# S5 matrices of a diffusion-transformer step: powers and B spread over partitions by DMA instead of transposes on TensorE

## Chip, cores and metric

One core of a Trainium2 chip runs the whole kernel in one launch. The metric is the time of one execution in device microseconds (us). A core has five engines that run side by side, each in the fixed order of its own instruction list: TensorE (PE, with PEld for its weight loads), VectorE (DVE), ScalarE (ACT), GpSimd (POOL) and SyncE (SP), which here issues nearly all DMAs.

## What is computed

The reference is one step of a four-layer backbone for 128 context and 512 latent tokens of width 1024. Layers 0 and 3 mix tokens by windowed attention, layer 2 by full attention, layer 1 by a bidirectional S5 layer; after each mixer stands a gated convolutional feed-forward network (FFN, width 2816). Each sub-layer is scaled, shifted and gated by a linear map of the conditioning ("modulation"). Of the S5 layer, cut to what matters here:

```
dt = exp(log_dt); mag = exp(lam_re*dt)
a  = mag * (cos(lam_im*dt) + i sin(lam_im*dt))      # per direction, 64 groups x 64 states
f  = (a - 1) / lam
bb = f * B                                          # 64 states x 16 channels, complex
h_t = a * h_(t-1) + bb @ u_t                        # scan forward, and a second one backward
y  = u*d_skip + sum over directions of Re(C h)
```

The kernel doesn't scan token by token. It works in chunks of eight tokens, and for this needs, per direction d and block of four group pairs (blk), matrices made of the powers a^0 to a^8 times bb or times C: an input matrix W (`d_w1`: from the 8 x 16 inputs of a chunk to the 64 complex states), an output matrix (`d_w3`, from P = C times powers) and a Toeplitz part inside the chunk (`d_kx`, from P times bb).

## The kernel before

Activations X lie in SBUF with channels on partitions. Every dense product is done in three f32 passes (`mm3`, L297 to L299): weights and inputs are split into a high and a low part, and hi*hi, hi*lo and lo*hi are added up. Weights come from DRAM through a pool of three raw tiles (`raw`, 1 MB each); ACT writes the high part `wh` (L302), DVE the low part `wl` (L306). PSUM tiles come from two pools, `psa` (two tiles) and `psb` (four banks). The build's scheduler fixes the order of each engine once; at run time each engine and each DMA queue goes through its list in that order and waits on semaphores. SP's list holds the weight loads, the loads and writes of the S5 work, and everything between.

The matrices of layer 1 don't depend on activations, and are made ahead, as side work between the matmuls of layer 0:

- `s5_param_steps` (a generator, three steps per chunk of w_o) runs in `project_out` of layer 0, about 306 to 365 us in the trace. It makes a and f for 64 (direction, pair) rows x 128 columns (`four`), transposes them on PE to 128 partitions, builds the powers `pw` (a^0 to a^8) by complex products (`cmul`, L1107 to L1113) on DVE, computes `bb` on DVE, and gathers powers, transposed C and bb in the tile `par`, one 392-wide row per step, written to DRAM as `d_par` (L1241). The last step loads the S5 start state and transposes it on PE (L1245, L1247).
- `s5_matrices` runs in `ffn` of layer 0, about 365 to 850 us, mixed three stages to one with the modulation products of the next layer. A step is one (blk, d), sixteen in all, each of four stages. Stage one loads `s5par` (L1265), makes P on DVE (real part) and POOL (imaginary part), three operations each (L1278 to L1280), writes it to `d_w3` (L1283) and builds the block-diagonal `bz` on ACT (L1292). Stage two multiplies P and bz on PE (L1299, eight products). Stage three copies the result to `kx`, and makes Q = bb times powers, three operations each on DVE and POOL (L1320 to L1322); Q lies state by input, and stands in the buffers that P had. Stage four transposes Q on PE (L1328, eight transposes of 128x128), and ACT evicts the four groups into W (L1331, with the sign of the imaginary part), which one DMA writes to `d_w1` (L1334). W and the scratch of both engines lie in one tile, `scr`.

The pools that these steps use have one buffer per name, so a step's P can't be made before the step before has used Q.

## Time and profile before

| | |
|---|---|
| median of 3 runs | 3241.3 us (3239.03 to 3242.83) |
| profiled execution | 3241.77 us, span 3240.0 us |
| mean granted TensorE clock | 0.982 of full speed |
| busy: PE / PEld / DVE / ACT / POOL | 97 / 91 / 67 / 43 / 16 % |
| chain of waits: PE / DVE / ACT / DMA / issue | 79 / 12 / 3 / 3 / 2 % |
| SP's DMA queue | 356.55 MB, 35.2 % of the 16 DMA engines' span |

The span is what the profile covers; the profiled execution's own time is 1.77 us longer. A busy share tells how full an engine is; the chain tells which work the end waited for, followed back from the last instruction. In a timeline row stand start, duration, engine, line, operation, output<-input, shapes and count, and in brackets how long the engine had been idle before and what released it. For DMA rows on SP ("SPq") the duration is that of issuing, not of the transfer; the page lists the time to landing apart. TensorE's clock has two levels, 1.2 and 2.4 GHz; the granted clock of a stretch is given as a share of the higher.

### The profile page before, as it was taken

Reading aid. Unit: us, or ns where it says so; the run is one execution under the profiler, and the core shown is the slowest. Engines: PE = TensorE matmul, PEld = TensorE weight load, DVE = VectorE, ACT = ScalarE, POOL = GpSimd, SP = SyncE. Lnnn points to the kernel's source line nnn. Section 1 sums busy time; section 2 is a strip of 40 time slices with the busy share of each in tenths; the row PEclk is TensorE's granted clock in tenths of the full one; section 3 lists DMA queues with packets and bytes.
Section 4 is the critical chain, followed back from the end, with each engine's and each line's share of the span. In section 5 each row is a group of like instructions: output and inputs, shape, how many; then the busy total and the mean of one; then the engine's idle time right before and its main releaser. Section 6 shows DMA issues by size and latency. Waiting matters only on the chain.

```text
span 3240.0 us, 55578 instructions
## 1 busy us (share of the span) xinstructions
PE 3127.2 (97%) x22620; PEld 2937.5 (91%) x22620; DVE 2156.8 (67%) x4114; ACT 1405.7 (43%) x2485; POOL 533.7 (16%) x916
## 2 busy tenths in 40 slices
PE   7999999989977999999999999999999999999999
PEld 6867999989956999999999889999999878999999
DVE  6666786796677368867766757677556775645543
ACT  4466443343441344433443654343344484533432
POOL 1332332353210000000013520000001431000000
PEclk8999999999987999999999999999999999999999
DMA  6251554444474424444431022434324212222221
GB/s 247 90 188 49 140 169 143 125 118 111 147 271 160 118 72 137 149 125 128 133 115 60 27 68 70 128 119 122 110 94 145 79 40 72 64 82 84 65 85 47
DMA packets 384288, 364.30 MB, mean 112 GB/s; under 512 B 39144, under 2 KB 357488, under 8 KB 374432
## 3 DMA queue, kind: packets, MB, share of 16 engines
q1 hardware_dynamic: 382752, 356.55, 35.2%
q8 instruction: 178, 2.92, 0.4%
q0 software_dynamic: 1280, 4.20, 0.4%
q14 instruction: 78, 0.64, 0.1%
HBM read 328.07 MB, written 36.83 MB: 113 GB/s over the span
## 4 chain that ended last, share of the span: by engine, by line
PE 79%; DVE 12%; ACT 3%; DMA 3%; issue 2%; POOL 1%; SPq 1%; DVEq 0%; ACTq 0%; POOLq 0%
PE psa L297 16%; PE psa L299 16%; PE psa L298 16%; PE psb L297 6%; PE psb L299 6%; PE psb L298 6%; PE psb L176 3%; PE psb L206 2%; DVE wl L306 2%; PE psb L440 1%; DVE Pt L1470 1%; PE psa L110 1%; PE psa L111 1%; ACT wh L302 1%; DVE H L1473 1%
## 5 line engine op out<-in xcount | busy, mean ns | idle before, releaser
L297 PE MATMUL psa<-yh,wh 128*128 128x384 f32 (+1 forms) x2752 | 854.3, 310 | 2.8 <-ACT hb L705 2.1
L299 PE MATMUL psa<-yh,wl 128*128 128x384 f32 (+1 forms) x2752 | 850.0, 309 | 0.0
L298 PE MATMUL psa<-yl,wh 128*128 128x384 f32 (+1 forms) x2752 | 849.7, 309 | 0.3 <-POOL yl L232 0.3
L306 DVE TENSOR_TENSOR wl<-raw,wh 128x2048 fp32r<-128x2048 f32 (+2 forms) x192 | 408.9, 2130 | 274.7 <-ACT wh L302 273.6
L297 PEld LDWEIGHTS psa<-yh,wh 128*128 128x128 f32 x2752 | 521.7, 190 | 19.1 <-issue 9.4
L302 ACT ACTIVATE wh<-raw 128x2048 fp32r<-128x2048 f32 (+2 forms) x192 | 333.1, 1735 | 465.7 <-PE psa L298 428.3
L298 PEld LDWEIGHTS psa<-yl,wh 128*128 128x128 f32 x2752 | 522.0, 190 | 0.5 <-POOL yl L232 0.5
L299 PEld LDWEIGHTS psa<-yh,wl 128*128 128x128 f32 x2752 | 521.7, 190 | 0.0
L297 PE MATMUL psa<-ah,wh 128*128 128x384 f32 (+1 forms) x1184 | 366.8, 310 | 7.4 <-DVE X L663 7.4
L299 PE MATMUL psa<-ah,wl 128*128 128x384 f32 (+1 forms) x1184 | 365.8, 309 | 0.0
L298 PE MATMUL psa<-al,wh 128*128 128x384 f32 (+1 forms) x1184 | 365.6, 309 | 0.0
L663 DVE SCALAR_TENSOR_TENSOR X<-psa,modt,X 128x256 f32<-128x256 f32 x372 | 141.6, 433 | 219.6 <-PE psa L299 219.6
L306 POOL TENSOR_TENSOR yl<-scr,yh 128x256 fp32r<-128x256 f32 (+1 forms) x36 | 41.5, 1154 | 1275.1 <-ACT yh L302 1249.1
L297 PEld LDWEIGHTS psa<-ah,wh 128*128 128x128 f32 x1184 | 224.2, 189 | 12.7 <-issue 7.3
L297 PE MATMUL psb<-wh,yh 128*128 128x256 f32 x800 | 228.2, 287 | 2.6 <-ACT yh L602 2.5
L299 PE MATMUL psb<-wh,yl 128*128 128x256 f32 x800 | 226.5, 286 | 1.8 <-POOL yl L306 1.6
L298 PE MATMUL psb<-wl,yh 128*128 128x256 f32 x800 | 226.9, 285 | 0.3 <-DVE wl L306 0.3
L298 PEld LDWEIGHTS psa<-al,wh 128*128 128x128 f32 x1184 | 224.3, 189 | 0.0
L299 PEld LDWEIGHTS psa<-ah,wl 128*128 128x128 f32 x1184 | 224.2, 189 | 0.0
L497 DVE SCALAR_TENSOR_TENSOR acc<-raw,cond,acc 128x512 f32<-128x512 f32 x280 | 197.3, 747 | 31.5 <-DMA raw<-in_w_mod_dram 31.3
L715 DVE SCALAR_TENSOR_TENSOR t<-hb,cols,t 128x641 f32<-128x641 f32 x176 | 170.7, 971 | 57.8 <-ACT t L713 57.8
L705 ACT ACTIVATE hb<-psa,cols 128x512 f32<-128x512 f32 x320 | 149.8, 519 | 124.7 <-PE psa L299 124.5
(320 smaller groups left out, 6254.2 us busy)
## 6 DMA issues: line engine op xcount, KB each, us to landing
raw<-in_w_up_dram SPq DMA_DIRECT2D x176, 512.0 KB, 5.1
raw<-in_w_mod_dram SPq DMA_DIRECT2D x80, 512.0 KB, 3.8
raw<-in_w_mod_dram SPq DMA_DIRECT2D x35, 1024.0 KB, 5.0
raw<-in_w_down_dram SPq DMA_DIRECT2D x48, 640.0 KB, 3.9
raw<-in_l_w_qkv_dram SPq DMA_DIRECT2D x20, 1024.0 KB, 6.0
raw<-d_w SPq DMA_DIRECT2D x16, 1024.0 KB, 4.8
raw<-in_w_down_dram SPq DMA_DIRECT2D x16, 896.0 KB, 4.6
raw<-in_l_w_o_dram SPq DMA_DIRECT2D x12, 1024.0 KB, 5.0
```

What stands on the lines that cost most here:

```text
L110: mm(out=out, lhsT=qt, rhs=kh, start=True, stop=False)
L176: nc.tensor.transpose(out=pt[:, o:o + 128], in_=self.Ps[g][:, c:c + 128], identity=K.ident)
L206: mm(out=po[64 * par:64 * par + 64, 0:256], lhsT=self.at.vraw[:, self.keys[i][b], self.kv * 64:self.kv * 64 + 64], rhs=PT[:, par], start=b ...
L297: mm(out=out, lhsT=wh, rhs=xh, start=start, stop=False)
L298: mm(out=out, lhsT=wh, rhs=xl, start=False, stop=False)
L299: mm(out=out, lhsT=wl, rhs=xh, start=False, stop=stop)
L302: self.nc.scalar.activation(out=out, in_=in_, func=ACTF.Copy)
L306: (sub or self.nc.vector).tensor_tensor(out=l, in0=x, in1=h.bitcast(F32), op=ALU.subtract)
L497: nc.vector.scalar_tensor_tensor(out=a, in0=st["w"][:, s], scalar=w, in1=a, op0=ALU.mult, op1=ALU.add)
L663: self.nc.vector.scalar_tensor_tensor(out=self.X[:, d, s0:s1], in0=p[:, o:o + s1 - s0], scalar=m[:, v, gate + d:gate + d + 1], in1=self.X[ ...
L705: nc.scalar.activation(out=hb[:, s0 + o - (s0 // 512) * 512:s1 + o - (s0 // 512) * 512], in_=p[:, b + s0:b + s1], func=ACTF.Identity, bias ...
L715: nc.vector.scalar_tensor_tensor(out=t, in0=hb[:, 0:641], scalar=kc[0], in1=t, op0=ALU.mult, op1=ALU.add)
```

## The change

In the parameter stage, powers a^0 to a^7 are also made in the layout of `four` (64 rows by 128 columns, tile `pq`: 18 DVE operations, a copy and two memsets) and written to DRAM by 16 DMAs (`d_pq`, L1205). `par` loses the powers for Q (32 POOL copies; 328 instead of 392 columns). After bb, 16 transposes on PE (L1258) and four evictions on ACT with scale -1 (L1261) bring bb, negated, to channel by state in a raw tile `bt`, which 16 DMAs write to DRAM (`d_bc`, L1265). d_par's write (L1267) and the state's load and transpose (L1271, L1273) follow.

In each step, Q, its eight transposes and its four evictions are gone. Instead 24 DMAs on SP bring the operands of W in W's own layout: eight spread `d_pq` over 16 partitions each (L1343, 64 KB), 16 repeat `d_bc` (L1346, 32 KB each; eight go into scr, eight into a buffer that P of this step had, named `s5Q`). Three operations each of 128x512 on DVE and POOL (L1355 to L1357) write W, and one DMA writes it to `d_w1` (L1358). The lines of the change are those of the changed kernel; what was L1247 is L1273 there, L1299 is L1323, L1283 is L1307, L1265 is L1291.

```diff
--- before.py
+++ after.py
@@ -1121,7 +1121,11 @@
         nc, i = self.nc, self.i
         v = nc.vector
         M, A_, S_ = ALU.mult, ALU.add, ALU.subtract
-        self.d_par = self.dram.tile([16, 128, 392], F32, name="d_par")
+        self.d_par = self.dram.tile([16, 128, 328], F32, name="d_par")
+
+
+        self.d_pq = self.dram.tile([2, 8, 2, 32, 128], F32, name="d_pq")
+        self.d_bc = self.dram.tile([2, 8, 2, 16, 4, 128], F32, name="d_bc")
         self.d_a8 = self.dram.tile([128, 2, 64], F32, name="d_a8")
         self.d_w1 = self.dram.tile([8, 128, 2048], F32, name="d_w1")
         self.d_w3 = self.dram.tile([8, 128, 2, 1024], F32, name="d_w3")
@@ -1187,6 +1191,19 @@
         v.tensor_copy(out=pw[:, 1], in_=p[:, 0:128].rearrange("p (r x) -> p r x", r=2))
         v.tensor_copy(out=ff, in_=p[:, 128:256].rearrange("p (r x) -> p r x", r=2))
         tmp = sp.tile([128, 1024], F32, name="tmp")
+
+        pq = sp.tile([64, 8, 2, 128], F32, name="pq")
+        nc.vector.memset(pq[:, 0, 0], 1.0)
+        nc.vector.memset(pq[:, 0, 1], 0.0)
+        v.tensor_copy(out=pq[:, 1], in_=four[:, 0:2])
+        for lo, n in ((1, 1), (2, 2), (4, 3)):
+            bc = lambda r: pq[:, lo, r].unsqueeze(1).to_broadcast([64, n, 128])
+            self.cmul(v, pq[:, lo + 1:lo + n + 1, 0], pq[:, lo + 1:lo + n + 1, 1], pq[:, 1:n + 1, 0],
+                      pq[:, 1:n + 1, 1], bc(0), bc(1), tmp[0:64, 0:n * 128].rearrange("p (k x) -> p k x", k=n))
+        for d in range(2):
+            for k in range(8):
+                nc.sync.dma_start(out=self.d_pq[d, k if d else 7 - k].rearrange("r x n -> x r n"),
+                                  in_=pq[32 * d:32 * d + 32, k])
         for lo in (1, 2, 4):
             bc = lambda r: pw[:, lo, r].unsqueeze(1).to_broadcast([128, lo, 64])
             self.cmul(v, pw[:, lo + 1:2 * lo + 1, 0], pw[:, lo + 1:2 * lo + 1, 1], pw[:, 1:lo + 1, 0],
@@ -1194,7 +1211,7 @@
         nc.sync.dma_start(out=self.d_a8, in_=pw[:, 8])
         yield
 
-        par = sp.tile([128, 16, 392], F32, name="par")
+        par = sp.tile([128, 16, 328], F32, name="par")
         for d in range(2):
             blks = slice(8 * d, 8 * d + 8)
             xs = slice(32 * d, 32 * d + 32)
@@ -1203,11 +1220,6 @@
                     k = q if d == 0 else 8 - q
                     src = pw[:, k, r, xs].rearrange("p (b g) -> p b g", g=4)
                     o = r * 36 + q * 4
-                    nc.gpsimd.tensor_copy(out=par[:, blks, o:o + 4], in_=src)
-                for q in range(8):
-                    k = 7 - q if d == 0 else q
-                    src = pw[:, k, r, xs].rearrange("p (b g) -> p b g", g=4)
-                    o = 72 + r * 32 + q * 4
                     nc.gpsimd.tensor_copy(out=par[:, blks, o:o + 4], in_=src)
         yield
 
@@ -1222,7 +1234,7 @@
                                         in_=ct[:, (4 * b4 + b) * 64:(4 * b4 + b + 1) * 64], identity=self.ident)
                 for t in range(2):
                     pv = p[0:64, :].rearrange("p (b g t c) -> p t b g c", b=4, g=4, t=2)[:, t]
-                    self.copy(par[t * 64:(t + 1) * 64, 4 * b4:4 * b4 + 4, 136 + r * 64:200 + r * 64]
+                    self.copy(par[t * 64:(t + 1) * 64, 4 * b4:4 * b4 + 4, 72 + r * 64:136 + r * 64]
                               .rearrange("p b (g c) -> p b g c", c=16), pv)
             yield
 
@@ -1236,8 +1248,22 @@
         bb = sp.tile([128, 2, 64, 16], F32, name="bb")
         self.cmul(v, bb[:, 0], bb[:, 1], bs[0], bs[1], fb(0), fb(1), tmp.rearrange("p (x c) -> p x c", c=16))
         for r in range(2):
-            nc.gpsimd.tensor_copy(out=par[:, :, 264 + r * 64:328 + r * 64],
+            nc.gpsimd.tensor_copy(out=par[:, :, 200 + r * 64:264 + r * 64],
                                   in_=bb[:, r].rearrange("p (b g) c -> p b (g c)", g=4))
+        bt = self.raw().rearrange("p (r b n) -> p r b n", r=2, b=8)
+        for r in range(2):
+            for h in range(2):
+                p = self.bankB()
+                for b in range(4):
+                    nc.tensor.transpose(out=p[:, b * 128:(b + 1) * 128],
+                                        in_=bb[:, r, 8 * (4 * h + b):8 * (4 * h + b + 1)].rearrange("p x c -> p (x c)"),
+                                        identity=self.ident)
+                nc.scalar.activation(out=bt[:, r, 4 * h:4 * h + 4], in_=p.rearrange("p (b n) -> p b n", b=4),
+                                     func=ACTF.Identity, scale=-1.0)
+        for x in range(8):
+            for r in range(2):
+                nc.sync.dma_start(out=self.d_bc[r, :, x // 4, :, x % 4].rearrange("b c n -> c b n"),
+                                  in_=bt[16 * x:16 * x + 16, r])
         nc.sync.dma_start(out=self.d_par.rearrange("b p x -> p b x"), in_=par)
         yield
 
@@ -1261,14 +1287,12 @@
                 nc.sync.dma_start(out=st["diag"], in_=self.i["diag16"])
                 st["scr"] = self.nrm.tile([128, 2560], F32, tag="scr", name="scr")
             scr = st["scr"]
-            pr = pool.tile([128, 392], F32, tag="s5par", name="s5par")
+            pr = pool.tile([128, 328], F32, tag="s5par", name="s5par")
             nc.sync.dma_start(out=pr, in_=self.d_par[8 * d + blk])
             w3p = [pr[:, r * 36:(r + 1) * 36].rearrange("p (q g) -> p g q", g=4).unsqueeze(3)
                    .to_broadcast([128, 4, 9, 16]) for r in range(2)]
-            w1p = [pr[:, 72 + r * 32:104 + r * 32].rearrange("p (q g) -> p g q", g=4).unsqueeze(3)
-                   .to_broadcast([128, 4, 8, 16]) for r in range(2)]
-            ct = [pr[:, 136 + r * 64:200 + r * 64].rearrange("p (g c) -> p g c", c=16) for r in range(2)]
-            bb = [pr[:, 264 + r * 64:328 + r * 64].rearrange("p (g c) -> p g c", c=16) for r in range(2)]
+            ct = [pr[:, 72 + r * 64:136 + r * 64].rearrange("p (g c) -> p g c", c=16) for r in range(2)]
+            bb = [pr[:, 200 + r * 64:264 + r * 64].rearrange("p (g c) -> p g c", c=16) for r in range(2)]
 
             P = [pool.tile([128, 4, 9, 16], F32, tag="s5P%d" % r, name="s5P") for r in range(2)]
             t = [scr[:, 1024 + 576 * r:1600 + 576 * r].rearrange("p (g q c) -> p g q c", q=9, c=16) for r in range(2)]
@@ -1311,26 +1335,26 @@
                                                in1=kx[:, 112:128], op0=ALU.mult, op1=ALU.add)
                 nc.sync.dma_start(out=self.d_kx[blk], in_=kx)
 
+            pq = scr[:, 1024:2048].rearrange("p (r n) -> p r n", r=2)
+            t2 = [pool.tile([128, 576], F32, tag="s5P%d" % r, name="s5Q")[:, 0:512] for r in range(2)]
+            nb = [scr[:, 2048:2560], t2[1]]
+            for q in range(8):
+                qs = slice(16 * q, 16 * q + 16)
+                nc.sync.dma_start(out=pq[qs], in_=self.d_pq[d, q, :, 4 * blk:4 * blk + 4]
+                                  .rearrange("r g n -> r (g n)").partition_broadcast(16))
+                for r in range(2):
+                    nc.sync.dma_start(out=nb[r][qs], in_=self.d_bc[r, 4 * d + blk // 2, blk % 2].rearrange("c g n -> c (g n)"))
+            yield
             W = scr[:, 0:1024].rearrange("p (q n) -> p q n", q=8)
-            b4 = [b.unsqueeze(2).to_broadcast([128, 4, 8, 16]) for b in bb]
-            Q = [pool.tile([128, 4, 8, 16], F32, tag="s5P%d" % r, name="s5Q") for r in range(2)]
+            Wr = [W[:, :, 64 * r:64 * r + 64] for r in range(2)]
+            g8 = lambda z: z.rearrange("p (g n) -> p g n", g=8)
+
+            tm = g8(t2[0]), g8(pq[:, 1])
             for r, eng in enumerate((nc.vector, nc.gpsimd)):
                 tt = eng.tensor_tensor
-                tm = t[r][:, :, 0:8]
-                tt(out=Q[r], in0=b4[0], in1=w1p[r], op=ALU.mult)
-                tt(out=tm, in0=b4[1], in1=w1p[1 - r], op=ALU.mult)
-                tt(out=Q[r], in0=Q[r], in1=tm, op=ALU.subtract if r == 0 else ALU.add)
-            yield
-            for h in range(2):
-                p = self.bankB()
-                for g in range(2):
-                    for r in range(2):
-                        nc.tensor.transpose(out=p[:, (r * 2 + g) * 128:(r * 2 + g + 1) * 128],
-                                            in_=Q[r][:, 2 * h + g].rearrange("p q c -> p (q c)"), identity=self.ident)
-                for r in range(2):
-                    nc.scalar.activation(out=W[:, 4 * h:4 * h + 4, r * 64:(r + 1) * 64],
-                                         in_=p[:, r * 256:(r + 1) * 256].rearrange("p (g n) -> p g n", n=64),
-                                         func=ACTF.Identity, scale=-1.0 if r else 1.0)
+                tt(out=Wr[r], in0=g8(nb[1 - r]), in1=g8(pq[:, 1]), op=ALU.mult)
+                tt(out=tm[r], in0=g8(nb[r]), in1=g8(pq[:, 0]), op=ALU.mult)
+                tt(out=Wr[r], in0=Wr[r], in1=tm[r], op=ALU.add if r else ALU.subtract)
             nc.sync.dma_start(out=self.d_w1[blk].rearrange("q (g d n) -> q g d n", d=2, n=128)[:, :, d], in_=W)
 
         def gather():
```

The change moves instructions on PE and SP. On PE, at the end of the second w_o chunk in `project_out` (psa is a product of the chunk, psb with wh the first half of the next one, raw the state), before:

```order
L297 MATMUL psa<-yh,wh 128x384
L298 MATMUL psa<-yl,wh 128x384
L299 MATMUL psa<-yh,wl 128x384
L1247 MATMUL psb<-ident,raw 128x128
L297 MATMUL psb<-yh,wh 128x256
L298 MATMUL psb<-yl,wh 128x256
L299 MATMUL psb<-yh,wl 128x256
```

and with the change:

```order
L297 MATMUL psa<-yh,wh 128x384
L298 MATMUL psa<-yl,wh 128x384
L299 MATMUL psa<-yh,wl 128x384
L1258 MATMUL psb<-ident,bb 128x128 x16
L1273 MATMUL psb<-ident,raw 128x128
L297 MATMUL psb<-yh,wh 128x256
L298 MATMUL psb<-yl,wh 128x256
L299 MATMUL psb<-yh,wl 128x256
```

The sixteen transposes of bb stand directly ahead of the state's transpose, between the same products.

On SP, in the parameter stage (in_state_l_dram is the start state, in_l_b the input B), before:

```order
L1232 DMA raw<-in_l_b_re_dram 128x64x16
L1232 DMA raw<-in_l_b_im_dram 128x64x16
L331 DMA raw<-in_l_w_o_dram 128x8x256
L1245 DMA raw<-in_state_l_dram 128x128
L1194 DMA d_a_3505<-pw 128x128
L329 DMA raw<-in_w_up_dram 128x8x128 x2
L1241 DMA d_par<-par 128x16x392
L329 DMA raw<-in_w_up_dram 128x8x128 x4
L1261 DMA s5diag<-in_diag_dram 128x16
L1265 DMA s5par<-d_par 128x392
```

and with the change:

```order
L1244 DMA raw<-in_l_b_im_dram 128x64x16
L1205 DMA d_pq<-pq 32x2x128 x6
L1211 DMA d_a_3507<-pw 128x128
L331 DMA raw<-in_l_w_o_dram 128x8x256
L1265 DMA d_bc<-raw 16x8x128 x16
L1267 DMA d_par<-par 128x16x328
L1271 DMA raw<-in_state_l_dram 128x128
L329 DMA raw<-in_w_up_dram 128x8x128 x6
L1287 DMA s5diag<-in_diag_dram 128x16
L1291 DMA s5par<-d_par 128x328
```

The state's load, which stood right behind the w_o load and ahead of d_par, now stands behind the 16 d_bc writes and d_par; all six w_up loads of this stretch follow it.

On SP, in the steps, around the third step (its two d_w3 writes are the first rows of L1283 behind d_kx), before:

```order
L1265 DMA s5par<-d_par 128x392
L331 DMA raw<-in_w_down_dram 128x5x256
L457 DMA raw<-in_w_mod_dram 128x2048
L1312 DMA d_kx<-s5kx 128x240
L1283 DMA d_w_3507<-s5P 128x4x128
L1334 DMA d_w_3506<-scr 1024x1x128
L1283 DMA d_w_3507<-s5P 128x4x128
L331 DMA raw<-in_w_down_dram 128x5x256 x2
```

and with the change, where the first three rows are the last of the 24 of that step's DMAs and the rest follow them:

```order
L1343 DMA scr<-d_pq 16x2x512
L1346 DMA scr<-d_bc 16x512
L1346 DMA s5Q<-d_bc 16x512
L457 DMA raw<-in_w_mod_dram 128x2048
L331 DMA raw<-in_w_down_dram 128x5x256
L1358 DMA d_w_3508<-scr 1024x1x128
L331 DMA raw<-in_w_down_dram 128x5x256 x2
L329 DMA raw<-in_w_up_dram 128x8x128 x4
```

The w_mod load stood ahead of the third step's d_w3 writes; now it and the w_down loads behind it stand behind all 24 DMAs of that step, which themselves stand behind its d_w3 writes.

## Rows read from the trace of the kernel before

**Rows 1.** The page: busy time and share per engine; the chain's share per engine.

```profile
PE 3127.2 (97%) x22620; PEld 2937.5 (91%) x22620; DVE 2156.8 (67%) x4114; ACT 1405.7 (43%) x2485; POOL 533.7 (16%) x916
...
PE 79%; DVE 12%; ACT 3%; DMA 3%; issue 2%; POOL 1%; SPq 1%; DVEq 0%; ACTq 0%; POOLq 0%
```

**Rows 2.** Busy time by stretch: length, PE, PEld, DVE, ACT, POOL, PE clock, DMA share, GB/s.

```profile
411.00:823.50 412.50, 398.38 (x2888) 380.69 (x2890) 316.02 (x336) 169.07 (x310) 157.98 (x105) 0.99 0.46 133
...
375.00:380.00 5.00, 5.00 (x25) 5.00 (x25) 3.05 (x4) 0.48 (x1) 0.00 (x0) 0.51 0.46 143
...
695.00:700.00 5.00, 5.00 (x30) 5.00 (x30) 4.38 (x4) 4.93 (x12) 4.92 (x3) 0.77 0.00 2
```

**Rows 3.** Waits of 365 to 850: total us, times, longest us (PE's; all engines').

```profile
PE psb L1328 <- DVE s5Q L1322: 5.7, 3, 2.4
...
POOL s5Q L1320 <- PE psb L1299: 169.2, 11, 39.8
```

**Rows 4.** Timeline, PE and PEld, a step of the matrices: start us, us, engine, line, operation.

```profile
424.06 0.33 PE L298 MATMUL psa<-yl,wh 128*128 128x384 f32 x1
...
424.23 0.33 PE L299 MATMUL psa<-yh,wl 128*128 128x384 f32 x1
...
426.84 0.97 PEld L1328 LDWEIGHTS psb<-ident,s5Q 128*128 128x128 f32 x8
...
427.77 0.19 PEld L297 LDWEIGHTS psa<-yh,wh 128*128 128x128 f32 x1
...
428.00 0.28 PE L298 MATMUL psa<-yl,wh 128*128 128x256 f32 x1
...
428.12 0.28 PE L299 MATMUL psa<-yh,wl 128*128 128x256 f32 x1
```

**Rows 5.** Line L1299 alone: ns min/median/max, first and last start us.

```profile
L1299 PE MATMUL psb<-s5P,s5bz x256: 272/273/300, 411.1 to 823.6; 128*32 128x128 f32 x128
```

**Rows 6.** Timeline, DMA issues on SP, parameter stage.

```profile
332.67 0.34 SPq L1245 DMA_DIRECT2D raw<-in_state_l_dram  x1
...
349.42 0.37 SPq L1241 DMA_DIRECT2D d_par<-par  x1
349.88 12.21 SPq L329 DMA_DIRECT2D raw<-in_w_up_dram  x4
```

**Rows 7.** Timeline, PE: the state's transpose; a wait in the norm (in brackets: idle before).

```profile
336.85 0.30 PE L1247 MATMUL psb<-ident,raw 128*128 128x128 f32 x1 [0.40 <-DMA raw<-in_state_l_dram]
...
371.19 0.38 PE L297 MATMUL psb<-yh,wh 128*128 128x256 f32 x1 [1.74 <-ACT yh L602]
```

**Rows 8.** Timeline, POOL, end of the parameter stage.

```profile
360.60 0.67 POOL L696 MEMSET hb<- 128x1 f32 x12 [11.21 <-DMA d_par<-par]
```

**Rows 9.** Timeline, DVE, powers and bb in the parameter stage.

```profile
329.54 1.23 DVE L1107 TENSOR_TENSOR bb<-raw,ff 128x1024 f32<-128x1024 f32 x1 [2.59 <-DMA raw<-in_l_b_re_dram]
...
332.56 0.43 DVE L1108 TENSOR_TENSOR tmp<-pw 128x256 f32<-128x256 f32 x1
...
339.92 1.22 DVE L1113 TENSOR_TENSOR bb<-bb,tmp 128x1024 f32<-128x1024 f32 x1
```

**Rows 10.** Timeline, SP: small loads early in the kernel; a d_w3 write of a step.

```profile
38.54 3.78 SPq L886 DMA_DIRECT2D gains<-in_l_q_norm_dram  x4
...
533.81 0.37 SPq L1283 DMA_DIRECT2D d_w<-s5P  x1
```

**Rows 11.** DMA issues by line: count, KB each, median us from issue to landing.

```profile
raw<-in_w_up_dram SPq DMA_DIRECT2D x176, 512.0 KB, 5.1
...
d_w<-s5P SPq DMA_DIRECT2D x32, 256.0 KB, 3.0
...
s5par<-d_par SPq DMA_DIRECT2D x16, 196.0 KB, 2.4
```

**Rows 12.** Groups by line and shape, 405 to 850: busy us, mean ns, idle before.

```profile
L306 DVE TENSOR_TENSOR wl<-raw,wh 128x2048 fp32r<-128x2048 f32 x19 | 49.7, 2614 | 16.2 <-ACT wh L302 16.2
...
L302 ACT ACTIVATE wh<-raw 128x2048 fp32r<-128x2048 f32 x19 | 36.4, 1914 | 44.2 <-PE psa L298 43.7 <-PE psb L298 0.4
```

## Prediction

> **What bounds the kernel now.** I read the busy shares and the chain of waits first. TensorE (PE) is busy 97 % of the span and carries 79 % of the chain; the chain's DVE share of 12 % is mostly the splitting of weights [rows 1]. So whatever takes PE's time or makes PE wait moves the end, and work on the other engines counts only where PE comes to wait for it. The profiled execution took 3241.77 us against a median of 3241.3; every sum below is made against 3241.8.
>
> Then the stage that the change works in, from the first to the last group of Toeplitz products (L1299) [rows 5]: 412.5 us with PE busy 398.4, so 14.1 idle, at a clock of 0.99 [rows 2]. There POOL is busy 158.0 us and ACT 169.1, so neither is near its limit. In the waits of this stage PE waits 5.7 us for the operands of the transposes, and POOL waits 169.2 us, in 11 places, for PE to reach L1299 [rows 3]: today the side work is ready and waits for PE. What it can be late by without harm is what the change has to fit into.
>
> **Removed from PE.** Eight transposes per step: their weight loads begin at 426.84 and the next product's at 427.77, so 0.93 us per step [rows 4], times 16 is 14.9 us. The 5.7 us of waits for their operands go too [rows 3]. The clock read 0.77 in 695 to 700 [rows 2], behind the longest of these waits, 2.4 us [rows 3]: about 5 x 0.23, 1.2 us, comes back. Sum -14.9 - 5.7 - 1.2 = -21.8; I take **-21 us**, since a PE that comes sooner meets the next late operand sooner. The four evictions of a step on ACT go at no gain, since ACT is busy 169 of 412 us [rows 2].
>
> **Unchanged.** DVE and POOL do three operations of 128x512 each per step as before. On POOL 32 small copies go; the d_par write waits for POOL today, but will wait for other work (next).
>
> **Added ahead of the steps, and the first stall.** PE's order puts the 16 new transposes (L1258) and the state's transpose (L1273) behind the second w_o chunk, where one transpose (L1247) stands today; everything that follows on PE, the last w_o halves first, is queued behind them. Today the state's load is issued at 332.67 and PE takes it at 336.85 after 0.40 us of waiting [rows 6, 7]. In the new order of SP this load stands behind 16 d_bc writes, which wait for the evictions of the new transposes, and behind d_par. Step by step:
> - DVE gets 18 more operations of 64 partitions, six each of widths 128, 256 and 384. At 256 one took 0.43 us, at 1024 1.23 [rows 9], so 0.30 and 0.56 at the other two: 7.7 us; as they overlap a little, an estimated 6.5. About 2 of it fit into DVE's 2.6 us of waiting for b_re [rows 9]. The last operation on bb begins at 339.92 and takes 1.22 [rows 9]; now it ends some 4.7 later, near 345.8.
> - The last eight transposes, 1.0, and two evictions, an estimated 1.4: 348.2.
> - 16 d_bc issues. A DMA of about this size took SP 0.37 us, one of a train of four small ones 3.78 / 4 = 0.95 [rows 10]. These have 16 partitions and few rows, like the first; with the gap to the next I take 0.40 to 0.42: 6.7 us, to 354.9. d_par and the state follow by 355.4.
> - d_par is 2.6 MB. Today's of 3.1 MB, issued at 349.42, landed 11.2 us later: POOL waited for it until 360.60 [rows 6, 8]. By bytes the new one takes 9.4, to 364.4. If the state's load, behind it in the same queue, lands only then, PE goes on at 364.5 instead of 336.85: **27.7 us**.
>
> Does a small load wait for the bytes ahead of it? The row that bears on it: four w_up loads issued behind d_par took SP 12.21 us to issue [rows 6], about the time of d_par's landing, so the queue was full of it. The Trainium skill, "DMA: Bandwidth & Descriptors", section "Queues, rings and completion order", says that on each DMA engine descriptors are consumed in ring order, though completion is not first in first out; by that the state lands behind d_par. The row points the same way. If the load overtook, it would land like a load of s5par, 2.4 us after its issue [rows 11], at 357.8: a stall of 21, and the sum 7 lower. If each d_bc cost 0.95, 8.5 more: 36.
>
> After this stall the clock is not whole: it read 0.51 in 375 to 380 [rows 2], behind a wait of 1.74 us [rows 7], which is 5 x 0.49 = 2.5 us lost. The 1.9 us of the 16 transposes lie inside the stall. First stage: 27.7 + 2.5 = **+30** (19 to 38).
>
> **Added in each step, and the second kind of stall.** 24 DMAs on SP: 24 x 0.40 = 9.6 us per step, 154 over the stage (0.37 each: 142; 0.95: 365). SP mostly waits in this stage today, but it works in order, and the train waits for this step's products and for d_w3 (the same buffers). Weight loads that stand behind the train are late by it. Where PE needs each, I counted in the new order of PE: a 384-wide product per 0.17 us (424.06 to 424.23), a 256-wide one per 0.12 (428.00 to 428.12) [rows 4]. A load behind the train comes 8.8 (22 DMAs behind the gate) + 0.4 to issue + 5.1 to land [rows 11] + 1.9 and 2.6 for the split [rows 12] = 18.8 us after the step's products. Counted from them, step 2 (of 0 to 15) needs its w_mod and w_down at 9.1 and 10.0, step 11 its w_up at 9.1, step 14 at 14.6: with w_down landing a little sooner 8.6, then 9.7, then 4.2, together 22.5 us.
>
> The other is the loop of a step: train 8.8, landing 2.4 (as s5par, [rows 11]), then POOL: busy 158.0 / 16 = 9.9 per step [rows 2], and 0.6 for starts: 21.7 us from one group of products to the next; and 25.4 where the products themselves were late, as then d_w3's issue (0.7) and landing, 3.0 [rows 11], come ahead. PE's work between groups in the new order is 14.3 to 43.3 us, with five intervals under 21.7: 19.6, 17.8, 16.3, 20.0 and 14.3. Leaving out 16.3, which step 11's stall covers, they lack 2.1 + 3.9 + 1.7 + 7.4 = 15.1. If all lateness is carried on it is up to 49, if the two kinds overlap fully about 20 in all.
>
> Sum of new stalls 37.5; five of these are over 2 us and each costs clock afterwards, an estimated 1.8, 9 us. Second stage: -21 + 37.5 + 9 = **+25.5**, with 20 to 60 for the stalls +5 to +50.
>
> **Sum.** 3241.8 + 30 + 25.5 = 3297.3: I forecast **3297**, as the median of runs is 0.5 under the profiled one; own range 3265 to 3330 (the lower and the upper ends of both stages). A change of 0.2 %, 6.5 us, is the least that measurements here can tell from none.
>
> **Rivals.**
> - *Only the first stall* (0.18). The steps' slack takes the trains: for it speaks POOL's 169 us of waiting for PE [rows 3]. Against it, in short intervals there is no such slack. 3241.8 + 30 - 21 = 3251 (3240 to 3260).
> - *Faster* (0.11). One mechanism: transposes tie PE to the step's chain, and without them the stage loses all that is not work: 14.9 + 14.1 idle [rows 2] + some 4 of clock = 33, the trains hidden, while the state's load overtakes d_par (21 + 2.5): 3241.8 + 23.5 - 33 = 3232. The point from which it decides: the stage's gain must pass the first stall by 6.5 us; with the stall at 30 it ends at 3239, which is no difference to be told. Against it: idle time for weights and residuals isn't the transposes' doing.
> - *All trains on the path* (0.11). SP is the bound of the stage, each train delaying the loads behind it: 3241.8 + 30 - 21 + 154 = 3405; at 0.37 each 3393, with a third of it hidden 3354. Against: most weights are loaded 20 to 50 us ahead. The Trainium skill, "VectorE: DVE Perf Modes", section "Rules for kernel authors", advises against this change: a 128x128 transpose belongs on TensorE where a PSUM destination will do. The trace agrees as far as queue time goes, 0.93 us of PE against 9.6 of SP; by the rule the sum is this one, by PE's slack 3297.
> - That the change doesn't do what it says is excluded by its order: the transposes of the steps are gone there.
>
> **Chances.** My forecast 0.60. Faster by over 0.2 %: 0.11 and the low end of the first rival, 0.13; within 0.2 % another part of it, 0.05; slower 0.82. The range leaves out the third case above and the second below, about 0.2: 3240 to 3350.
>
> **What would show it.** Right: PE idle some 20 to 30 us ahead of L1273, released by the state's DMA, which SP issued near 355; no PE waits for s5Q; in the steps POOL's or DVE's W operations waiting for the trains and PE waiting for split weights in steps 2 and 11 and for products late in steps 10, 14 and 15; each new DMA at about 0.40 us of SP. Wrong: the state's wait under 10 us, or bb done much before 345; trains over 12 us or under 7; the stage from the first to the last L1323 shorter than 398 or longer than 460.

## The result, and the profile after

The changed kernel takes 3429.0 us (median of four, 3427.7 to 3431.7) against 3240.5 of the kernel before: the ratio is 1.058, 95 % interval 1.057 to 1.060. It is slower, as forecast, but by 189 us instead of 57, and outside the range.

The page of the changed kernel (span; busy time and share of each engine; the chain's share per engine), which answers to [rows 1]:

```profile
span 3425.3 us, 55838 instructions
...
PE 3153.0 (92%) x22508; PEld 2956.8 (86%) x22508; DVE 2150.1 (63%) x4135; ACT 1397.0 (41%) x2425; POOL 526.7 (15%) x884
...
PE 77%; DVE 10%; DMA 4%; ACT 3%; POOL 3%; issue 2%; SPq 1%; DVEq 0%; POOLq 0%; ACTq 0%
```

PE is busy 26 us more although 112 matmuls are gone, and its share fell from 97 to 92 %: it waits 160 us more, and part of its work ran at the lower clock. Where this begins and ends is read from the products of the steps, the line of [rows 5] (times in ns, then first and last start):

```profile
L1323 PE MATMUL psb<-s5P,s5bz x256: 269/417/423, 433.0 to 1008.0; 128*32 128x128 f32 x128
```

The first products come at 433.0 instead of 411.1 us (+21.9), the last ones 575.0 us after them instead of 412.5 (+162.5), and from there to the end it is 2417.3 against 2416.4. These three make the 185 us between the two spans. Busy time by stretch, as in [rows 2] (length, PE, PEld, DVE, ACT, POOL, PE clock, DMA share, GB/s):

```profile
433.00:1008.00 575.00, 427.81 (x2819) 404.58 (x2820) 314.83 (x348) 164.98 (x259) 151.35 (x105) 0.84 0.43 121
599.00:615.00 16.00, 16.00 (x109) 16.00 (x108) 10.00 (x14) 8.49 (x16) 2.16 (x2) 1.00 0.27 87
621.20:624.00 2.80, 2.76 (x24) 1.44 (x24) 1.84 (x1) 0.00 (x0) 1.15 (x1) 0.50 0.26 72
```

**The first stretch.** SP's issues and PE's rows at the new transposes (in brackets: idle before, and what ended it):

```profile
343.45 10.04 SPq L1265 DMA_DIRECT2D d_bc<-raw  x16
353.59 0.39 SPq L1267 DMA_DIRECT2D d_par<-par  x1
354.08 2.86 SPq L1271 DMA_DIRECT2D raw<-in_state_l_dram  x1
357.04 12.53 SPq L329 DMA_DIRECT2D raw<-in_w_up_dram  x6
```

```profile
340.85 1.94 PE L1258 MATMUL psb<-ident,bb 128*128 128x128 f32 x8 [5.06 <-DVE bb L1109]
343.91 1.94 PE L1258 MATMUL psb<-ident,bb 128*128 128x128 f32 x8 [1.11 <-DVE bb L1113]
364.38 0.45 PE L1273 MATMUL psb<-ident,raw 128*128 128x128 f32 x1 [18.53 <-DMA raw<-in_state_l_dram]
```

PE waits 5.06 + 1.11 us for bb, and 18.53 for the state, which was issued at 354.08, behind the 16 d_bc writes and d_par, and taken at 364.38. The prediction had 355.4 and 364.5.

**The steps.** PE's waits from the first to the last products (total us, times, longest), then SP's and POOL's:

```profile
PE psb L1323 <- DVE s5P L1304: 89.1, 11, 14.7
PE psa L297 <- ACT wh L302: 31.3, 6, 10.2
PE psa L299 <- DVE wl L306: 9.9, 8, 3.8
```

```profile
SPq L1358 <- DVE scr L1357: 175.3, 15, 19.9
SPq L1307 <- POOL s5P L1304: 45.5, 13, 6.2
SPq L1358 <- POOL scr L1357: 38.3, 15, 3.6
```

```profile
POOL scr L1355 <- DMA s5Q<-d_bc: 195.0, 15, 18.1
POOL scr L1356 <- DVE scr L1355: 141.4, 15, 17.5
```

PE waits 147 us here (575.0 - 427.8) where it waited 14: 97 of it at the products (89.1 for DVE's P, 2.2 for POOL's, and 5.8 in one wait that the profile puts down to a split of the FFN on ACT), 41 for split weights. SP stands 214 us at the d_w1 write, waiting for W; POOL waits 141 us, 15 times, for DVE's half of W: POOL's second product is put into the half of the tile `pq` that DVE's L1355 still has to read. One step shows how that goes, first SP, then POOL, then DVE, then PE:

```profile
586.35 0.97 SPq L1307 DMA_DIRECT2D d_w<-s5P  x1
587.37 1.08 SPq L1343 DMA_DIRECT2D scr<-d_pq  x1
...
599.40 0.42 SPq L1346 DMA_DIRECT2D s5Q<-d_bc  x1
599.92 0.37 SPq L1291 DMA_DIRECT2D s5par<-d_par  x1
600.33 1.11 SPq L457 DMA_DIRECT2D raw<-in_w_mod_dram  x1
617.64 0.53 SPq L1358 DMA_DIRECT2D d_w<-scr  x1
```

```profile
602.51 1.30 POOL L1355 TENSOR_TENSOR scr<-scr 128x512 f32<-128x512 f32 x1 [15.15 <-DMA s5Q<-d_bc]
...
614.13 1.74 POOL L1356 TENSOR_TENSOR scr<-s5Q,scr 128x512 f32<-128x512 f32 x1 [10.32 <-DVE scr L1355]
```

```profile
610.99 0.89 DVE L715 SCALAR_TENSOR_TENSOR t<-hb,cols,t 128x641 f32<-128x641 f32 x1 [1.42 <-ACT t L713]
...
612.71 0.69 DVE L1356 TENSOR_TENSOR s5Q<-scr 128x512 f32<-128x512 f32 x1
...
614.04 0.69 DVE L1357 TENSOR_TENSOR scr<-scr,s5Q 128x512 f32<-128x512 f32 x1
614.76 1.73 DVE L1302 TENSOR_TENSOR s5P<-s5par 128x576 f32<-128x576 f32 x1
617.65 1.75 DVE L1303 TENSOR_TENSOR scr<-s5par 128x576 f32<-128x576 f32 x1 [1.16 <-POOL scr L1357]
619.44 1.66 DVE L1304 TENSOR_TENSOR s5P<-s5P,scr 128x576 f32<-128x576 f32 x1
```

```profile
621.24 0.39 PE L1323 MATMUL psb<-s5P,s5bz 128*32 128x128 f32 x1 [5.19 <-DVE s5P L1304]
```

The train of 24 DMAs is issued from 587.37 to 599.82, 12.5 us. POOL has its data at 602.51, but DVE comes to W (L1355 to L1357) only at 612.71: in its order W stands behind the FFN's convolution (L715, L717), whose inputs PE is still making; PE is busy all of 599 to 615. Then W, and P of the next step right behind it, take from 612.7 to 621.1, and now it is PE that stands, at L1323, for 5.19 us; after that its clock is down (0.50 in 621.2 to 624, the lower level; 1.00 in 599 to 615). SP meanwhile waits from 601.4 to 617.6 at d_w1, with the weight loads behind it.

### The profile page after: what moved, and what is told of

The parts are those of the page before. It is cut to its first block, busy times and chain, and to the rows that moved or that the text cites. A ratio compares the mean times of both kernels' runs of the same rounds, so it can differ in the third digit from the quotient of the medians.

```text
span 3425.3 us, 55838 instructions
## 1 busy us (share of the span) xinstructions
PE 3153.0 (92%) x22508; PEld 2956.8 (86%) x22508; DVE 2150.1 (63%) x4135; ACT 1397.0 (41%) x2425; POOL 526.7 (15%) x884
## 4 chain that ended last, share of the span: by engine, by line
PE 77%; DVE 10%; DMA 4%; ACT 3%; POOL 3%; issue 2%; SPq 1%; DVEq 0%; POOLq 0%; ACTq 0%
PE psa L297 16%; PE psa L299 16%; PE psa L298 16%; PE psb L297 6%; PE psb L299 6%; PE psb L298 6%; PE psb L176 2%; PE psb L206 2%; PE psb L440 1%; DVE wl L306 1%; PE psa L110 1%; DVE Pt L1494 1%; PE psa L111 1%; DVE H L1497 1%; DVE Tt L1496 1%
## 5 line engine op out<-in xcount | busy, mean ns | idle before, releaser
L306 DVE TENSOR_TENSOR wl<-raw,wh 128x2048 fp32r<-128x2048 f32 (+2 forms) x192 | 407.2, 2121 | 310.0 <-ACT wh L302 286.2
L297 PE MATMUL psa<-ah,wh 128*128 128x384 f32 (+1 forms) x1184 | 373.4, 315 | 12.5 <-ACT wh L302 7.6
L715 DVE SCALAR_TENSOR_TENSOR t<-hb,cols,t 128x641 f32<-128x641 f32 x176 | 159.4, 907 | 174.6 <-ACT t L713 174.4
L306 POOL TENSOR_TENSOR yl<-scr,yh 128x256 fp32r<-128x256 f32 (+1 forms) x36 | 41.3, 1151 | 1275.6 <-ACT yh L302 1120.8
```

What stands on the lines that cost most here:

```text
L297: mm(out=out, lhsT=wh, rhs=xh, start=start, stop=False)
L306: (sub or self.nc.vector).tensor_tensor(out=l, in0=x, in1=h.bitcast(F32), op=ALU.subtract)
L715: nc.vector.scalar_tensor_tensor(out=t, in0=hb[:, 0:641], scalar=kc[0], in1=t, op0=ALU.mult, op1=ALU.add)
```

## The experiments

All times stand beside runs of the kernel before in the same session (3239 to 3241 us). "First stretch" is what happens up to the first products, "stage" the time from the first to the last products.

The scheduler makes the orders of the engines anew for each version, and they come out differently. Counted in the traces, the matmuls of other work that stand between one group of products and the next are the same in the kernel before, `e_params`, `e_ctrl`, `e_fake4` and `e_own_fake4`; `e_state` has those of the changed kernel; `e_split`, `e_w1pool`, `e_own` and the runs with the train in the old steps each have others. Between the ninth and the tenth group, for instance, stand 95 in the kernel before and in `e_fake4`, 159 in the changed kernel, 190 in `e_dfree`. What these runs change is therefore the edit together with the orders that follow from it.

**The first stretch alone** (`e_params`). The kernel before, and from the change only this:

```diff
+ pq powers on DVE, 16 writes d_pq
+ 16 transposes of bb, 4 evictions, 16 writes d_bc   (ahead of d_par and the state)
  the sixteen steps as before
```

> The kernel before with the additions to the parameter stage alone (powers pq, their writes, transposes of bb, d_bc writes), whose results nothing reads; the sixteen steps are those of before. It prices the first stage alone. The starts of the Toeplitz products moved by 21.9 us between the two kernels (411.1 to 433.0), so 3240.5 + 22 = 3262 (3255 to 3270). If the steps of before soak up part of it in their slack (POOL waits 169 us for PE there), less. Rival: the stage's lateness also upsets the steps (weights late at their start), and the time is over 3280.

Measured: 3268.0 us, ratio 1.009 (1.007 to 1.010), +28 us; PE waits 19.8 us for the state there. Its stage takes 412.9 us, as before. So the first stretch costs 28 of the 189 us, and the other 161 are the steps' (by the spans of the changed kernel 22 and 163).

**The state's load early** (`e_state`).

```diff
+ st = self.raw(); load of state_l1; transpose; s0     (ahead of the loads of B)
  ...
- st = self.raw(); load of state_l1; transpose; s0     (behind d_par)
```

> The changed kernel with one edit: the load and the transpose of the S5 start state stand ahead of the loads of B, so ahead of the d_bc writes and of d_par on SP, and ahead of the transposes of bb on PE. If the 18.5 us that PE waits at the state's transpose are real path, they go, and some clock behind them: 3429 - 18.5 - 3 = 3407 (3400 to 3415). The 6.2 us of waiting for bb at its transposes stay. Rival: the wait only moves, to w_up weights that are loaded after it or to s5par, and the time stays above 3420.

Measured: 3418.9 us, 10 less, not 22. The 18.5 us of waiting are gone, but PE's waits in 300 to 440 us now read:

```profile
PE psb L1267 <- DVE bb L1109: 6.1, 1, 6.1
PE psb L297 <- ACT wh L302: 3.2, 1, 3.2
PE psb L1267 <- DVE bb L1113: 2.0, 1, 2.0
PE psb L299 <- DVE wl L306: 1.6, 1, 1.6
```

The waits for bb grew by 2, and 4.8 us of waiting for the last w_o weights came out from behind the stall. Half of what was removed had been cover for something else.

**A short train** (`e_fake4`): 24 DMAs become 4, with the same bytes, buffers and operations; it leaves out the spreading, so W's values are not the right ones.

```diff
- for q in range(8): 3 DMAs of 16 partitions
+ for r in range(2):
+     dma(pq[:, r] <- d_pq[d] as [128, 512]); dma(nb[r] <- d_bc[r, 4d:4d+4] as [128, 512])
```

> The changed kernel, but each step's operands come by 4 DMAs instead of 24: two of 128x512 from d_pq, two of 128x512 from d_bc, the same 1 MB into the same buffers. The spreading is left out: the values are not those that W needs. Theory A, the loop: the steps are bound by a closed chain (products, train of DMAs, W, P, next products) through shared buffers, of which the train's 12.6 us are a third; with some 2.0 us instead the mean interval falls from 38.3 to 27.7 us against 23.9 of PE's own work, so the stage from the first to the last products takes 400 to 440 us instead of 575, and the kernel 3270 to 3300. Theory B, the head of SP's queue: what costs is that the d_w1 write stands ahead of weight loads on SP and waits there for W on DVE, 213 us in all; that stays as it is, and the time stays over 3370.

Measured: 3285.8 us, 143 less. Its products, and PE's longest waits in its stage:

```profile
L1323 PE MATMUL psb<-s5P,s5bz x256: 269/273/423, 432.4 to 863.5; 128*32 128x128 f32 x128
```

```profile
PE psa L297 <- DVE X L663: 15.8, 3, 6.3
PE psb L1323 <- DVE s5P L1304: 10.4, 4, 3.5
```

The stage takes 431.1 us instead of 575.0, and the waits for P fell from 89.1 to 10.4. 20 DMAs less per step, at the 0.47 us from one start to the next, are 16 x 20 x 0.47 = 150 us. That this is so near the 143 us is in part chance: with the short train PE waits only 34 us in the stage (431.1 less 397.1 of work), so its own work is the bound there and not the loop, and PE's and DVE's orders changed too. In the changed kernel DVE begins W on average 10.4 us after the last issue of the train, in `e_fake4` 1.0 us. What is shown is that with the short train, and the orders that go with it, nearly all of the loss is gone. The heads of queues (theory B) would have left the time over 3370.

**Half the train on another queue** (`e_split`).

```diff
- nc.sync.dma_start(...)                          # 24 a step
+ (nc.sync, nc.scalar)[q % 2].dma_start(...)      # 12 from SP, 12 from ACT
```

> The changed kernel, the 24 DMAs of a step shared between two issuing engines: those of even q from SP, those of odd q from ACT, 12 each; nothing else. Theory A, the loop: the train is half as long (6 instead of 12.6 us), so up to 6 us go from each of the 15 intervals of 38.3 us, and some clock with them: 3429 - 95 = 3335 (3310 to 3365). Rival: the number of DMAs is what costs, wherever they are issued (the DMA engines take so long for them), or ACT, held in order by the waits of its 12 DMAs, is late with the evictions that PE waits for: 3390 or more.

Measured: 3314.9 us, 114 less, with the same number of DMAs and the same bytes. PE's waits for P in its stage:

```profile
PE psb L1323 <- DVE s5P L1304: 42.1, 11, 7.5
```

Neither the DMA engines nor the count as such are the limit; how long one engine needs to issue the train is. By the issue times alone, 16 x 12 x 0.47, it would be 90 us; DVE, which now begins W 2.4 us after the last issue in place of 10.4, may give back the rest.

**d_w1 from another engine** (`e_w1pool`).

```diff
- nc.sync.dma_start(out=self.d_w1[blk]...)
+ nc.gpsimd.dma_start(out=self.d_w1[blk]...)
```

> The changed kernel with the d_w1 write of each step issued by POOL instead of SP, so that SP is not held by it (213 us of SP waiting go). Theory A, the loop: only PE's waits for split weights go, 31.3 + 9.9 + 4.9 us, and some clock: 3429 - 45 to 60, 3370 to 3395, while PE goes on waiting about 90 us for P at the products. Theory B, the head of SP's queue: most of the stage's 162 us come back, 3280 to 3310.

Measured: 3393.4 us, 36 less. SP's longest wait in the stage is now another one:

```profile
SPq L1307 <- DVE s5P L1304: 201.1, 15, 22.2
```

The wait has moved from d_w1 to the next step's d_w3 write, for P, and is almost as long as before (201 us against 214). PE's waits for P are 56.5 us there in place of 89.1, those for weights 35 in place of 41. SP's wait at d_w1 is a consequence: whatever waits first behind a late W takes it over. The time is where theory A had it, but not by its way: the waits for weights, which it had going, stayed, and those for P, which it had staying, fell.

**The shared buffers** (`e_ctrl`, `e_own`, `e_own_w1pool`). The memory comes from cutting layer 0's FFN into five phases; `e_ctrl` is the kernel before with that alone.

```diff
- bounds = (0, 5, 10, 15, 22)                   # actp: 7 buffers
+ bounds = (0, 5, 10, 15, 20, 22) if l == 0 else (0, 5, 10, 15, 22)     # actp: 5 if l == 0
  e_own, on the changed kernel:
- t2 in P's buffers ("s5P%d"); P's scratch t in scr[:, 1024:2176]
+ t2 in tiles of its own ("s5T%d"); t in tiles of its own ("s5U%d")
```

> A control for the next two: the kernel before with the first layer's FFN in five phases of at most five tiles instead of four of at most seven (bounds 0, 5, 10, 15, 20, 22), which frees 10 KB per partition. PE's products are the same; one more phase adds eight more residual updates on DVE. 3240 to 3255.

> The changed kernel with those five phases and with the memory they free: the operand and product tiles of W no longer stand in P's buffers, and P's scratch no longer in that of W's operands, so a step's train and the next step's P wait for no buffer of each other; all 24 DMAs stay on SP. Theory A1, the loop closes through the shared buffers: without them the train runs while PE does its 24 us per step, PE's 90 us of waiting for P mostly go, and the stage falls from 575 to 420 to 470 us: 3290 to 3330. Theory A2, the loop is closed by the engines' orders as well (in DVE's order P of the next step still stands right behind W in most steps, and W waits for the train): the stage stays over 500 us, the time over 3355.

Measured: the control 3255.3 (+15), `e_own` 3414.6; if the control's 15 add up, that is 3400, some 30 us under the changed kernel. PE's waits in the stage of `e_own`:

```profile
PE psa L297 <- ACT wh L302: 48.6, 10, 7.3
PE psa L299 <- DVE wl L306: 39.2, 10, 8.7
PE psb L1323 <- DVE s5P L1304: 16.2, 5, 6.2
```

The wait for P fell as expected, 89 to 16 us, but most of that was not won: the wait for split weights rose from 41 to 88. The loads stand behind the train on SP. POOL's second product still stands in `pq` here, and POOL waits 73 us for DVE's L1355; no run gave that product a tile of its own. With d_w1 on POOL as well:

> e_own with the d_w1 writes issued by POOL. In e_own PE's waits for P fell from 89 to 16 us, but its waits for split weights rose from 41 to 92: the weight loads stand on SP behind the trains and behind d_w1, where SP waited 130 us for W. Theory D, SP's order: with d_w1 away SP is held less and the weight waits fall by more than half, 92 to under 45 us, and the time from 3415 to 3345 (3320 to 3370). Theory E, SP's plain occupation: 24 issues of 0.46 us per step in front of the loads are enough to make them late; then the weight waits stay over 70 us and the time over 3390.

Measured: 3393.6; in 300 to 1010 us the waits for weights are 89 us (54.3 + 34.9) where `e_own` has 92 in the same stretch. Theory D, that SP's waiting at d_w1 makes the weights late, falls, and the figures are those of theory E. But SP waits as long in the stage as before, 281 us against 275, now at d_w3, d_kx and the train instead of d_w1; so this run does not tell SP's occupation from its waiting in order at some other write.

**The same train in the old steps** (`e_dfree`, `e_dloop`, `e_dloop2`, `e_dload`). Each is the kernel before with its transposes, plus 24 DMAs of 32 KB per step on SP; they differ in who waits for them. Two smaller differences: the DMAs of `e_dfree`, in pieces of 512 bytes, took SP 0.59 us each (median) and those of the other three 0.42, and `e_dload` does Q in the stage of the transposes.

```diff
+ for n in range(24):
+     e_dfree:   d_junk[...] <- d_w3 of this step          # no buffer waits
+     e_dloop:   d_junk[...] <- rows of P                  # Q waits (P's buffers)
+     e_dloop2:  d_junk[...] <- rows of Q                  # the next P waits (Q's buffers)
+     e_dload:   scratch of Q, Q[1] <- rows of a weight    # Q's operations wait
```

> The same 24 DMAs of 32 KB per step on SP at the same place, but their source is what d_w3 has just written to DRAM, so that no buffer and no engine waits for them: SP is occupied as long, the chain is not longer. Theory A: SP's slack of some 25 us per step takes 11 us and what they wait for; weights come late in a few places: 3240 to 3275. Theory E, SP's plain occupation ahead of the weight loads is what costs: as slow as its twin with the DMAs in the chain, over 3300, with PE waiting for split weights.

> The kernel before, with transposes and all, plus 24 DMAs of 32 KB per step on SP that write rows of P to a DRAM buffer which nothing reads. They stand right behind d_w3 and read P's buffers, so Q, which takes these buffers, waits for them: a train of the length of the change's, put into the closed chain of before and with nothing else of the change. Theory A, the loop: products, 24 issues of 0.46 (11 us), landing 2, Q 5, transposes and evictions, P 5.5 make 27 us or more against PE's 25.8 per step, and with the orders of the engines more: the stage grows by 40 to 160 us, 3280 to 3400, with PE waiting for P at the products. Theory F, the change's own operations (W's reads of DMA-loaded tiles in DVE's and POOL's orders) cost: under 3265.

> The kernel before plus the same 24 DMAs of 32 KB per step on SP, now behind Q: they read Q's rows, so they wait for the products and Q, and P of the next step, which takes Q's buffers, waits for them. In e_dloop the train ran between P and the products, beside PE's own work ahead of them, and cost 70 us; here it stands in the same place of the chain as in the changed kernel (products, operands of W or Q, train, P, products), with s5par behind it on SP. Theory A, place in the chain: it now costs what the change does, less the first stage and with the transposes still there: 3239 + 130 to 180 = 3370 to 3420, with PE waiting some 80 us for P at the products. Theory E, SP's occupation is all: as the other two, 3295 to 3320, and then the rest of the change's loss lies in W's operations and their waits for the loads.

> The kernel before plus 24 DMAs of 32 KB per step on SP that load rows of a weight into the scratch of Q's operations and into Q's own buffer, ahead of these operations, which then overwrite them: so DVE's and POOL's Q wait for the train to land, as W does in the changed kernel; the transposes follow Q in the same stage, as d_w1 follows W. Theory G, operations that wait for loads: it is this wait in DVE's and POOL's fixed orders, and what is queued behind it (d_w1 and the weight loads on SP, P, the products), that makes the rest of the change's loss: 3241 + 120 to 180, 3360 to 3420. Theory E: as in the three runs with the train elsewhere, 3295 to 3320.

Measured: 3297.1, 3310.1, 3296.0 and 3310.4 us: +58, +71, +55 and +70. `e_dloop` alone lies where theory A (the train's place in the chain) has it; but `e_dfree`, where no buffer waits, is nearly as slow, and in `e_dloop2` theory A missed by 74 us and more (3370 to 3420), in `e_dload` theory G (operations that wait for loads) by 50 and more (3360 to 3420). Where the train stands in the chain makes 15 us here; that SP is occupied by it, with what then comes late behind it, makes 55. In `e_dfree` that is not the weights, for which PE waits 0.8 us in the stage: its largest wait there is 28.3 us for P, and P's own load `s5par` stands on SP behind the train:

```profile
POOL s5P L1279 <- DMA s5par<-d_par: 248.4, 13, 30.4
```

So the loop can close there too, through SP's order, and the run does not price SP's occupation alone. But the changed kernel's steps lose 161. The stages of `e_dload` and of `e_dfree`, whole:

```profile
410.90:912.50 501.60, 461.15 (x3199) 438.48 (x3198) 320.38 (x367) 190.36 (x330) 147.46 (x105) 0.96 0.49 139
```

```profile
410.00:906.20 496.20, 452.52 (x3205) 432.00 (x3204) 334.39 (x371) 192.91 (x331) 157.00 (x105) 0.98 0.50 146
```

They are long as well, about 500 us against 412.5. But PE did some 3200 matmuls in them, where in the stage before it did 2888, 120 of them the steps' transposes, and in the changed kernel's 2819. So these two hold some 310 matmuls more than the stage before, at the mean of 0.138 us (398.4 / 2888) about 43 us of the FFN's work, which otherwise came later; the changed kernel's stage holds only 51 more than before, its transposes set aside. In the fixed order of `e_dfree` and `e_dload` there is more other work of PE between the products than in the changed kernel's, and PE waits less. That this is why the same train costs them 60 and the change 161 was not tried by itself, and one trace speaks against it. The stage of `e_w1pool`:

```profile
434.30:999.20 564.90, 465.00 (x3086) 438.00 (x3088) 335.86 (x371) 176.91 (x271) 155.17 (x120) 0.90 0.45 130
```

It holds 3086 matmuls, none of them the steps' transposes, as much other work of PE as `e_dfree` (3205 - 120 = 3085). Yet PE waits 99.9 us in it where it waits 43.7 in `e_dfree`, and the kernel is 153 us slower than the one before. More work between the products is thus not enough; why the same train costs the old steps so much less stays open.

**Versions with fewer or divided DMAs** (`e_rep_state`, `e_rep_late`, `e_own_split_late`, `e_own_fake4`). The first two spread once, by writes that POOL issues in the parameter stage, and load 4 whole tiles per step; `late` puts the transposes of bb behind four halves of w_o.

```diff
  e_rep_state:
+ gpsimd: d_pq[...] <- pq repeated 16 times; d_bc[...] <- bt repeated 8 times    # 8 MB each
+ 4 DMAs of 128 x 512 a step; state early
  e_rep_late:       + bb's transposes, d_bc and d_par at half(6, 0)
  e_own_split_late: e_own + e_split + state early + late
  e_own_fake4:      e_own + e_fake4 + state early + late
```

> A complete version of the 4-DMA kernel: the spreading is done once, in the parameter stage, where POOL issues writes of pq repeated 16 times and of bb's transposes repeated 8 times to DRAM (8 MB each); a step then loads whole 128-partition tiles with 4 DMAs. The state's load stands early, as in e_state. If the 4-DMA kernel's time is the count of DMAs in the loop and nothing of its false values, this is 3286 less the 10 us of e_state: 3276, plus what 16 MB of writes between 310 and 400 us cost: 0 to 25 us. 3270 to 3300. Rival: the writes hold the weights in the DMA engines so that PE waits in 340 to 430: over 3310.

> As e_rep_state, and the transposes of bb (with their writes and d_par) stand four halves of w_o later in PE's order, where bb is long done. In e_state PE still waited 8.1 us for bb at these transposes and 4.8 for the next weights: these should go, 3276 - 10 = 3265 (3250 to 3290). Rival: s5par and the operands come later by as much as the transposes, the first steps start late, and nothing is gained over e_rep_state.

> All that helped at once: own buffers with five phases, the train shared between SP and ACT, the state's load early and the transposes of bb four halves later. With the train halved (e_split: 3315), the first stall mostly gone (10 to 18) and some of the 42 us of PE's waits for P in e_split gone: 3270 (3240 to 3295). Under A2 own buffers add nothing: 3290 to 3305.

> The bound of what the idea can give here: own buffers with five phases, 4 DMAs of whole tiles per step (the spreading is left out, W's values are not the right ones), the state's load early and the transposes of bb late. Neither the loop nor SP's train is left; what should remain is the control (3255) with the first stage some 11 us longer and the steps shorter by the transposes, up to 15: the stage from first to last products 395 to 405 us against the control's 410, the time 3253 (3243 to 3268). If it is over 3275, something else in the new steps costs (W's operations on DVE and POOL, or the bytes).

Measured: 3359.9, 3359.5, 3278.8 and 3298.3 us. `e_rep_late` gains nothing on `e_rep_state`. The steps of `e_rep_state` are nearly as short as those of `e_fake4` (first to last products 500.9 to 939.3, 438 us against 431); what it loses, it loses ahead of them. Waits of all engines in 300 to 450 us:

```profile
ACT wh L302 <- DMA raw<-in_w_up_dram: 36.7, 1, 36.7
...
PE psb L297 <- ACT yh L602: 35.4, 1, 35.4
...
PE psb L1268 <- DVE bb L1109: 32.8, 1, 32.8
...
DVE bb L1107 <- DMA raw<-in_l_b_re_dram: 29.0, 1, 29.0
```

These are 32 writes of 512 KB, 16 for each of the two tensors. The first operation on B waited 29.0 us for its load, which was under way together with the d_pq writes, and the split of a weight 36.7 us for one that was under way together with the d_bc writes. `e_own_split_late` is the best complete version, and still 38 us over the kernel before (ratio 1.012, 1.011 to 1.014), of which its control explains 15. `e_own_fake4` missed its 3253 by 45 us: there PE waits for evictions on ACT (25.6 us) and for residuals (15.6) instead; what makes these late was not followed up. It is also 19 us slower than `e_own_split_late`, which has the same buffers and 24 DMAs over two queues instead of 4 on SP: between these two the train's length does not decide. None of the versions beats the kernel before.

## Why the prediction was wrong

*The first stretch: right.* +30 was forecast (19 to 38), `e_params` measures +28. The sequence held: bb late, 16 writes, d_par, the state behind it. That it held nearly to the microsecond (364.5 forecast, 364.38 measured) is luck, since two errors cancel: the d_bc writes took 10.0 us instead of 6.7, as the second waited until 346.5 for the last evictions (L1261), but they began 4.7 us earlier. PE's wait came in three pieces, 5.06 + 1.11 + 18.53 = 24.7 us, where one of 27.7 was forecast. The small load was held by the bytes ahead of it, as forecast: PE took the state 10.3 us after its issue.

*What the transposes give back: right in the direction, not measured by itself.* No run took the transposes away without a train. `e_fake4` comes closest: 18 us over `e_params` with 4 DMAs per step, so the new steps, even with a short train, don't return the 15 us.

*The trains: the step that failed.* It is the sum for "the loop of a step" (train 8.8, landing 2.4, POOL 9.9, starts 0.6), 21.7 us from one group of products to the next. Measured, it is 575.0 / 15 = 38.3 us. Three things were missing in it. First the size of the train: 12.5 us in the step shown, for the issues came 0.47 apart and all 24 count. Then, and more, W was reckoned on POOL alone, and to begin when the data land; in fact POOL's second operation waits for DVE, and DVE's half stands in its order behind FFN work: 141 us of POOL's time. In the step shown, 35.2 us long (586.07 to 621.24), the time from the data to the next products is 18.7 us (602.51 to 621.24) where 9.9 + 0.6 stood, so this term lacks 8.2 us and the train 3.7. Last, the loop and the late weights were added up as if one step's lateness ended with it, "they lack 15.1"; measured, PE waits 97 us at the products and 41 for weights, and the lateness is carried from step to step: the period over all fifteen is the 38.3 us.

*The clock: too small.* 9 us were taken. PE's 2819 matmuls of the stage kept it busy 427.8 us, the 2888 of before 398.4; less the transposes' 14.9 and with 51 other matmuls more, about 9 us, that would be an estimated 392 at the old clock. The other 35 us are the lower clock (0.84 of the higher level against 0.99): as in the row at 621.2 to 624, stretches at a lower clock follow the waits.

*The rivals.* "All trains on the path", 3405 at a chance of 0.11, came nearest, and still 24 us short. That the trains are on the path is shown by `e_fake4` (143 us less with 4 DMAs) and `e_split` (114 less with two queues). Its mechanism, loads delayed behind each train, is only a part: of PE's 147 us of waits in the stage 41 are for split weights and 97 stand at the products. In the old steps the same train cost 55 to 71 us; where the other 100 us or so come from stays open, since the count of other matmuls between the products does not explain it (`e_w1pool`). Against this rival I had set that "most weights are loaded 20 to 50 us ahead", counted in the order of PE's work; a queue that falls 12 us behind in each step would use that up in some three steps.

*The signs.* Slower at 0.82 was right, and "Faster" is excluded. "Only the first stall" (3251) falls by 178 us. Two of the signs named for being wrong came: the stage over 460 us (575.0) and trains over 12 us (12.5). One reading was wrong without bearing on the sum: the splitting of weights is not most of DVE's 12 % of the chain, for the page gives `wl` on L306 2 %.

The Trainium skill's rule that had been weighed ("VectorE: DVE Perf Modes", "Rules for kernel authors": a 128x128 transpose belongs on TensorE where a PSUM destination will do) held here: the 0.93 us per step on PE that it would have kept were cheaper than what replaced them.

## What to carry to other kernels

A train of small DMAs is a serial piece of work on the engine that issues it, here 0.47 us each whatever the size between 32 and 64 KB: multiply by the count, and ask first what else must go through that engine in the same interval. The scheduler may also set new orders around it; compare these before putting a time difference down to the train itself. Where the new operands come by DMA, walk the whole cycle through buffers, queues and every engine's order once round, and compare it with the work that the bottleneck has in between; if it is longer, the difference comes back in every turn and with the clock on top. And when a stall is taken out, look at what had been late behind it: the state's 18.5 us gave back 10.

## What the runs showed of the hardware that I had not expected

- The same 24 DMAs, shared between SP's and ACT's queues, cost 114 us less than from SP alone, so two engines issue side by side (12 each in place of 24), and ACT had the room. The engines' orders changed with it, so not all of the 114 us are issue time.
- An issue on SP took 0.42 us for 32 KB and for 64 KB in 16 partitions; with the gap, 0.47. The d_bc writes of 64 KB, in pieces of 512 bytes, took SP 0.43 us each, `e_dfree`'s from DRAM to DRAM in pieces of 512 bytes 0.59.
- While 16 writes of 512 KB each, issued from POOL, were under way, operations waited up to 36.7 us for loads issued from SP (`e_rep_state`). A second queue was no protection from the first one's bytes.
- With 112 matmuls fewer PE was busier, 3153 against 3127 us: the clock in the steps was 0.84 of the higher level instead of 0.99.
